# One value product of 256 columns for both parts of the attention weights, and attention outputs stored as two parts in block order

## The chip, the cores and the metric

The kernel runs as one launch on one core of a Trainium2 chip. The metric is the device time of that launch in microseconds; of several runs the median is taken. A profile is one further execution, recorded by the hardware profiler. Engines are called as in the profile: PE (TensorE, products), PEld (its weight loads), DVE (VectorE), ACT (ScalarE), POOL (GpSimd), SP (SyncE, which here only issues DMAs).

## What is computed

One layer of a hybrid encoder on 1024 tokens (a grid of 16 rows of 64) with 1024 channels: a half feed-forward step, a token mixer of two branches (neighbourhood attention and a state-space model, SSM), a second half feed-forward step, an embedding step and a final norm. All of it is float32. The change lies in the attention branch and, with a few lines, in the final norm. Cut to these:

```python
def neighbourhood_attention(q, k, v, rpb):        # 8 heads of 64 channels
    def row_block(r):
        rs = jnp.clip(r - wh // 2, 0, rows - wh)                   # window of 8 rows
        kr = lax.dynamic_slice_in_dim(kg, rs, wh, axis=1)
        vr = lax.dynamic_slice_in_dim(vg, rs, wh, axis=1)
        kn = kr[:, :, col_idx]                                     # 16 columns for each query
        vn = vr[:, :, col_idx]
        ...
        sc = jnp.einsum('bchd,brcwhd->bhcrw', qr, kn) * scale + bias[None]
        pr = jax.nn.softmax(sc, axis=-1)...
        return jnp.einsum('bhcrw,brcwhd->bchd', pr, vn)
...
        y_attn = neighbourhood_attention(q, k, v, na_rpb[i]) @ w_attn_out[i]
        y_ssm = s5_branch(s_in, ...) @ w_ssm_out[i]
        h = h + (g_attn * y_attn + g_ssm * y_ssm) @ w_out[i]
...
    return rms_norm(h, final_norm)
```

## The kernel before

**Products in two parts.** Operands of the large products are split into a high part, rounded to the type float32r, and a low part, the rest. A product is then the sum of high x high, high x low and low x high, three products in one accumulator (`mm3`, L183 to L186; `split`, L152 to L154, writes the high part on ACT and the low part on DVE).

**The mixer.** Two streams of work are woven together on PE. The outer one is a plain sequence of projections: the SSM input, the values (stored to v_d), then for each pair of heads the queries and keys (`qk_proj`) and the gates (`gate_tile`, L1360). After each `mm3` it calls `tick()`. The inner one is the generator `mixer_side` (L1287), which hands out a piece of attention or of the SSM each time its count of ticks has run out. PE executes in the order in which the program is written; the other engines' instructions are put in order by a scheduler.

**Attention.** A unit is one head, one half of the grid's rows (rb) and one of four column blocks (cb) of 16 columns: 128 queries against 12 rows of 24 or 32 keys. There are 8 x 2 x 4 = 64 units. Round j of the loop at L1319 does four things in this order: the scores of unit j (`attn_scores`: two products into the tile s, the table added and the minimum taken on DVE, the exponential and its scaling on ACT), the transposes of unit j - 3 (`attn_turn`: three on PE into the tile pt, then the high part pth by ACT and the low part ptl by DVE), the value products of unit j - 5 (`attn_values`), and two steps of the SSM scan on POOL. From round 48 on (SO) it adds the SSM outputs: `ssm_out` copies states out of the scan's array (xs, L1111) and three rounds later runs products into yo. A round ends with 4 ticks (from 48 on 3), that is 12 (9) products of 512 columns of the outer stream.

The value products need high x high, high x low and low x high. PE's loaded operand holds 64 high and 64 low columns of the values (vhl), so one product with pth over these 128 columns gives high x high in partitions 0 to 63 and low x high in 64 to 127; a second one with ptl, over the 64 high columns alone, adds high x low to the former:

```python
            T.matmul(O[:, ksl(cb)], lhsT=hl[0:kp, rb + g].rearrange("p h d -> p (h d)"), rhs=ph[0:kp, ksl(g)], start=(g == 0), stop=False,
            T.matmul(O[0:64, ksl(cb)], lhsT=hl[0:kp, rb + g, 0], rhs=pl[0:kp, ksl(g)], start=False, stop=(g == 2),
```

With three groups g of four rows that is six products a unit. O is one PSUM bank (of 8, all under one tag) for four units; after the fourth, ACT copies its lower half out (ol), DVE adds the halves in row order (ot), and ACT's queue stores 64 x 512 numbers to o_d, of shape 512 x 1024.

**Reading the outputs back.** When the inner stream has ended, `load_br` (L1400) reads o_d (b = 0) and the SSM branch's y2_d (b = 1) for the two halves t of the tokens, through buffers "st" (three, 1024 columns each) and "tmp" (four, 512 columns), and splits them into bh and bl for the products br (`branches`). Between these reads SP issues those of the residual (hbuf from h_d), of the weights (wst from in_was) and stores of gates (g_d).

**Buffers.** While the mixer runs, "w" (12 of 1024 columns) holds weights, queries and keys, "x" (56 of 512 columns) everything else of that width.

**The end.** `end` (L1675) writes the last quarter of the embedding and the final norm by hand: the order on DVE and ACT there is that of the program. `stat` gathers the squares on PE (ms), `rstd` (L205) makes the reciprocal root from ms, `scaled` (L1654) multiplies by the last gain on ACT, `finish` multiplies and stores.

## Time and profile before

| | |
|---|---|
| time, median of 3 runs | 2098.58 us (2096.72 to 2100.43) |
| time of the profiled execution | 2096.29 us |
| span of the profiled execution | 2094.5 us, 28063 instructions |
| mean granted TensorE clock | 0.998 |
| attention units (value products) | 851.7 to 1104.5 us of the span |
| HBM read, written | 201.01 MB, 82.31 MB |

The span is the time from the first to the last instruction; the execution's own time also holds what lies around it, 1.8 us. The page cuts the span into 40 equal slices of 52 us; a digit is the busy share of a slice in tenths, so that the mixer is to be seen in the middle, from where POOL works a second time (the SSM scan):

```profile
PE   8999999999999999999999999999999999999998
DVE  7897776667967334677753668995665665786855
ACT  6434333334445333667774635643333334445543
POOL 0037556441000006888200001000000000000000
```

A row of a tile or of a line gives the number of instructions, the shortest, median and longest duration in ns and the first and last start in us. A row of the timeline gives start, duration, engine, line, operation, out<-in, and in brackets the idle time before it and what ended it. Starts of products lie closer together than their durations, since products are pipelined.

### The profile page before, as it was taken

What the parts mean: (1) busy time and instruction counts of PE and PEld (TensorE: products, weight loads), DVE (VectorE), ACT (ScalarE), POOL (GpSimd) and SP (SyncE); (2) the same over time, 40 slices, a digit from 0 to 9 for tenths busy, and PEclk for the clock granted to TensorE, in tenths of its full rate; (3) what the DMA queues carried; (4) which work ended last, traced back from release to release, by engine and by line L of the source; (5) the groups of instructions that cost most, each with busy time, mean ns of one, the idle gap of its engine ahead of it and who ended that gap; (6) DMA issues with size and microseconds to landing.
All of it is one profiled execution on the core that took longest, in us unless ns stands there. A gap on an engine that the chain in (4) does not pass through costs nothing.

```text
span 2094.5 us, 28063 instructions
## 1 busy us (share of the span) xinstructions
PE 2074.5 (99%) x9662; PEld 1705.4 (81%) x9662; DVE 1416.1 (68%) x2420; ACT 999.6 (48%) x1832; POOL 399.4 (19%) x636
## 2 busy tenths in 40 slices
PE   8999999999999999999999999999999999999998
PEld 3788888888888888888898888788888888888886
DVE  7897776667967334677753668995665665786855
ACT  6434333334445333667774635643333334445543
POOL 0037556441000006888200001000000000000000
PEclk9999999999999999999999999999999999999999
DMA  3435444475533551233477745243324238433302
GB/s 134 143 118 154 125 135 120 144 270 169 188 114 111 159 189 64 70 97 98 123 208 260 247 145 117 77 150 121 100 86 135 82 121 297 155 106 94 118 21 81
DMA packets 197744, 285.19 MB, mean 136 GB/s; under 512 B 41569, under 2 KB 81121, under 8 KB 197601
## 3 DMA queue, kind: packets, MB, share of 16 engines
q1 hardware_dynamic: 180304, 258.20, 38.8%
q10 hardware_dynamic: 14992, 21.00, 3.0%
q0 software_dynamic: 2304, 4.20, 1.2%
q8 instruction: 76, 1.25, 0.2%
q14 instruction: 68, 0.55, 0.1%
HBM read 201.01 MB, written 82.31 MB: 135 GB/s over the span
## 4 chain that ended last, share of the span: by engine, by line
PE 94%; DVE 2%; ACT 1%; DMA 1%; SPq 0%; issue 0%; DVEq 0%; ACTq 0%
PE dx L184 4%; PE dx L185 4%; PE dx L186 4%; PE gx L184 3%; PE ux L184 3%; PE ux L186 3%; PE gx L186 3%; PE gx L185 3%; PE ux L185 3%; PE gt L184 3%; PE gt L185 3%; PE gt L186 3%; PE dy L186 2%; PE dy L184 2%; PE dy L185 2%; PE gy L184 2%
## 5 line engine op out<-in xcount | busy, mean ns | idle before, releaser
L153 ACT CAST wh<-hbuf 128x512 fp32r<-128x512 f32 x280 | 173.0, 622 | 392.3 <-PE gx L185 80.9
L154 DVE TENSOR_TENSOR wl<-hbuf,wh 128x512 fp32r<-128x512 f32 x280 | 209.2, 750 | 122.7 <-ACT wh L153 120.5
L153 ACT CAST wh<-wblk 128x512 fp32r<-128x512 f32 x190 | 118.0, 622 | 192.6 <-PE dx L185 83.2
L154 DVE TENSOR_TENSOR wl<-wblk,wh 128x512 fp32r<-128x512 f32 x190 | 130.6, 690 | 49.3 <-ACT wh L153 41.8
L184 PE MATMUL dx<-ah,wh 128*128 128x512 f32 x416 | 163.3, 393 | 0.3 <-DVE hbuf L688 0.3
L186 PE MATMUL dx<-ah,wl 128*128 128x512 f32 x416 | 161.9, 389 | 0.0
L185 PE MATMUL dx<-al,wh 128*128 128x512 f32 x416 | 161.8, 389 | 0.0
L1092 POOL TENSOR_TENSOR sc<-X,rho 128x128 f32<-128x128 f32 x128 | 77.9, 609 | 327.2 <-ACT X L1075 317.3
L154 DVE TENSOR_TENSOR al<-araw,ah 128x512 fp32r<-128x512 f32 x154 | 106.3, 694 | 50.1 <-PE dx L185 21.1
L184 PE MATMUL gx<-xh,wh 128*128 128x512 f32 x320 | 124.9, 390 | 1.2 <-DVE c L575 1.2
L184 PE MATMUL ux<-xh,wh 128*128 128x512 f32 x320 | 125.0, 390 | 0.0
L186 PE MATMUL ux<-xh,wl 128*128 128x512 f32 x320 | 124.5, 389 | 0.0
L185 PE MATMUL gx<-xl,wh 128*128 128x512 f32 x320 | 124.5, 389 | 0.0
L186 PE MATMUL gx<-xh,wl 128*128 128x512 f32 x320 | 124.5, 389 | 0.0
L185 PE MATMUL ux<-xl,wh 128*128 128x512 f32 x320 | 124.5, 389 | 0.0
L153 ACT CAST ah<-araw 128x512 fp32r<-128x512 f32 x154 | 94.9, 619 | 43.2 <-PE dx L185 12.6
L184 PE MATMUL gt<-xh,wh 128*128 128x512 f32 x256 | 102.7, 401 | 0.0
L186 PE MATMUL gt<-xh,wl 128*128 128x512 f32 x256 | 99.8, 390 | 0.0
L185 PE MATMUL gt<-xl,wh 128*128 128x512 f32 x256 | 99.8, 390 | 0.0
L422 DVE TENSOR_TENSOR hbuf<-hbuf 128x512 f32<-128x512 f32 x120 | 91.4, 762 | 2.1
L184 PEld LDWEIGHTS dx<-ah,wh 128*128 128x128 f32 x416 | 78.1, 188 | 17.8 <-issue 0.7
L185 PEld LDWEIGHTS dx<-al,wh 128*128 128x128 f32 x416 | 78.1, 188 | 16.9 <-issue 0.7
(381 smaller groups left out, 5590.2 us busy)
## 6 DMA issues: line engine op xcount, KB each, us to landing
araw<-a_d SPq DMA_DIRECT2D x154, 256.0 KB
a_d<-c SPq DMA_DIRECT2D x148, 256.0 KB
wblk<-in_wd SPq DMA_DIRECT2D x88, 256.0 KB
hbuf<-in_wg SPq DMA_DIRECT2D x40, 512.0 KB
hbuf<-in_wu SPq DMA_DIRECT2D x40, 512.0 KB
wst<-in_win SPq DMA_DIRECT2D x26, 512.0 KB
hbuf<-in_xT SPq DMA_DIRECT2D x32, 256.0 KB
h_d<-hbuf ACTq DMA_DIRECT2D x32, 256.0 KB
```

Source lines behind the costliest of these rows:

```text
L153: A.copy(hi, src)
L154: return eng.tensor_tensor(lo, src, hi.bitcast(F32), ALU.subtract)
L184: T.matmul(o, lhsT=wh, rhs=xh, start=first, stop=False, skip_group_check=more)
L185: T.matmul(o, lhsT=wh, rhs=xl, start=False, stop=False, skip_group_check=more)
L186: T.matmul(o, lhsT=wl, rhs=xh, start=False, stop=last, skip_group_check=more)
L422: V.tensor_tensor(b11, (b12, b22, None, None, b21)[i - 2], b11, ALU.subtract)
L1092: G.tensor_tensor(sc, both, rho4, ALU.mult)
```

## The change

**One product for both parts.** `attn_turn` writes the high and the low part of the transposed weights side by side into one tile ptb (three groups of 2 x 128 columns, two buffers). `attn_values` loads all 128 columns of vhl and streams 256 columns in one product a group: three a unit. It also gives low x low, which is not used.

**Two column blocks in a bank.** O is a bank for two units now, each with 256 columns; 32 banks are taken instead of 16. After the second unit ACT copies the columns that belong to the high part (all 128 partitions) into ot, DVE adds the high x low part to partitions 0 to 63, and ot is stored as it is: 2 x 64 x 256 numbers to o_d, which is 2 x 512 x 1024 now, in the order of the column blocks. The sum of the two halves and the order by rows are made when it is read back: `load_br` reads both halves into two "st" buffers, adds them on DVE, and the split reads the sum in the changed order.

**Order in a round.** The value products stand ahead of the transposes.

**Buffers.** The queries are kept in 512-wide buffers, one for each half of the tokens, and "w" has 10 buffers instead of 12.

**The end.** In the last `stat`, the two scalings come after the reciprocal root on ACT (`mid`).

```diff
     v_d = dtile("v_d", [SEQ, 512])
-    o_d = dtile("o_d", [512, SEQ])
+    o_d = dtile("o_d", [2, 512, SEQ])
     g_d = dtile("g_d", [16, P, SEQ])
...
-    def rstd(m, r, q):
+    def rstd(m, r, q, mid=None):
         A.activation(r, m, AF.Abs_reciprocal_sqrt, bias=eps)
+        if mid is not None:
+            mid()
         V.tensor_tensor(q, r, r, ALU.mult)
...
-        def stat(self, r=None, summed=False):
+        def stat(self, r=None, summed=False, mid=None):
             if summed:
...
             r = thid("rs", [P, self.n], F32) if r is None else r
-            rstd(m, r, q)
+            rstd(m, r, q, mid)
             self.r = r
...
     ap_ = ap_cm.__enter__()
-    cur.update(st=(ap_, "st", 3), w=(ap_, "w", 12), tmp=(ap_, "tmp", 4))
+    cur.update(st=(ap_, "st", 3), w=(ap_, "w", 10), tmp=(ap_, "tmp", 4))
...
             for i in range(2):
-                if t == 0:
-                    qs.append(tw("qs"))
+                q = thid("qs")
+                qs.append(q)
                 src = o[i * 64:(i + 1) * 64].rearrange("p (r b c) -> p r b c", r=8, b=4)
...
                 def view(sl):
-                    return qs[i][sl, hsl(t)].rearrange("p (b r c) -> p r b c", b=4, r=8)
+                    return q[sl].rearrange("p (b r c) -> p r b c", b=4, r=8)
                 A.copy(view(hs), src)
...
         for i in range(2):
-            qkv[2 * hp + i] = (qs[i], kh[i], kl[i])
+            qkv[2 * hp + i] = (qs[i::2], kh[i], kl[i])
...
         nk = 12 * n
-        qv = q[:, rb * HT + cb * P:rb * HT + (cb + 1) * P]
+        qv = q[rb][:, ksl(cb)]
...
             T.transpose(tp[0:kp, ksl(g)], sm[:, g * kp:(g + 1) * kp], ident)
-        ph = thid("pth", [P, 384])
-        pl = thid("ptl", [P, 384])
-        A.copy(ph[0:kp], tp[0:kp, 0:384])
-        V.tensor_tensor(pl[0:kp], tp[0:kp, 0:384], ph[0:kp].bitcast(F32), ALU.subtract)
-        return ph, pl
-    def attn_values(hd, rb, cb, O, ph, pl):
+        pb = ap_.tile([P, 3, 2, P], F32R, tag="ptb", bufs=2, name="ptb")
+        src = tp[0:kp, 0:384].rearrange("p (g q) -> p g q", g=3)
+        A.copy(pb[0:kp, :, 0], src)
+        V.tensor_tensor(pb[0:kp, :, 1], src, pb[0:kp, :, 0].bitcast(F32), ALU.subtract)
+        return pb
+    def attn_values(hd, rb, cb, O, pb):
         kp = 4 * KNC[cb]
         hl = vld[hd, cb]
+        o = O["o"][:, (cb % 2) * 256:(cb % 2) * 256 + 256]
         for g in range(3):
-            T.matmul(O[:, ksl(cb)], lhsT=hl[0:kp, rb + g].rearrange("p h d -> p (h d)"), rhs=ph[0:kp, ksl(g)], start=(g == 0), stop=False,
+            T.matmul(o, lhsT=hl[0:kp, rb + g].rearrange("p h d -> p (h d)"), rhs=pb[0:kp, g].rearrange("p h q -> p (h q)"), start=(g == 0), stop=(g == 2),
                      skip_group_check=True)
-            T.matmul(O[0:64, ksl(cb)], lhsT=hl[0:kp, rb + g, 0], rhs=pl[0:kp, ksl(g)], start=False, stop=(g == 2),
-                     skip_group_check=True)
-        if cb == 3:
-            ot, ol = tmp("ot"), tmp("ol")
-            A.copy(ol[0:64], O[64:128])
-            V.tensor_tensor(ot[0:64].rearrange("p (r b c) -> p b r c", r=8, b=4),
-                            O[0:64].rearrange("p (b r c) -> p b r c", b=4, r=8),
-                            ol[0:64].rearrange("p (b r c) -> p b r c", b=4, r=8), ALU.add)
-            nc.scalar.dma_start(o_d[hd * 64:(hd + 1) * 64, hsl(rb)], ot[0:64])
+        if cb % 2 == 0:
+            return
+        ot = ap_.tile([P, 256], F32, tag="ot", bufs=2, name="ot")
+        ov = ot.rearrange("p (b q) -> p b q", b=2)
+        src = O["o"].rearrange("p (b h q) -> p h b q", b=2, h=2)
+        A.copy(ov, src[:, 0])
+        V.tensor_tensor(ov[0:64], src[0:64, 1], ov[0:64], ALU.add)
+        nc.scalar.dma_start(o_d[:, hd * 64:(hd + 1) * 64, rb * HT + (cb - 1) * P:rb * HT + (cb + 1) * P], ot)
...
                 sms[j] = attn_scores(hd, rb, cb)
+            if 0 <= j - 5 < n:
+                hd, rb, cb = units[j - 5]
+                if cb % 2 == 0:
+                    O.setdefault((hd, rb), {})["o"] = bank("O")
+                attn_values(hd, rb, cb, O[hd, rb], pts.pop(j - 5))
+                if rb == 1 and hd + 1 < NH:
+                    load_v(hd + 1, cb)
             if 0 <= j - 3 < n:
                 pts[j - 3] = attn_turn(units[j - 3][2], sms.pop(j - 3))
-            if 0 <= j - 5 < n:
-                hd, rb, cb = units[j - 5]
-                if cb == 0:
-                    O[hd, rb] = bank("O")
-                attn_values(hd, rb, cb, O[hd, rb], *pts.pop(j - 5))
-                if rb == 1 and hd + 1 < NH:
-                    load_v(hd + 1, cb)
             scan_steps(2)
...
             for k in range(0, 4, 2):
-                st = tst("br")
-                nc.sync.dma_start(st.rearrange("p (k c) -> p k c", k=2),
-                                  o_d[k * P:(k + 2) * P, hsl(t)].rearrange("(k p) c -> p k c", p=P))
+                st = [tst("br") for _ in range(2)]
+                for w in range(2):
+                    nc.sync.dma_start(st[w].rearrange("p (k c) -> p k c", k=2),
+                                      o_d[w, k * P:(k + 2) * P, hsl(t)].rearrange("(k p) c -> p k c", p=P))
+                V.tensor_tensor(st[0], st[0], st[1], ALU.add)
                 for i in range(2):
                     hi, lo = tx("bh"), tx("bl")
-                    split(hi, lo, st[:, hsl(i)])
+                    sv = st[0][:, hsl(i)].rearrange("p (b r c) -> p r b c", b=4, r=8)
+                    hv, lv = (x.rearrange("p (r b c) -> p r b c", b=4, r=8) for x in (hi, lo))
+                    split(hv, lv, sv)
                     res.append((hi, lo))
...
         A.activation(dummy, eps, AF.Abs_reciprocal_sqrt)
-        scaled(6, six[3])
         added(a, b, s, hm)
         fin[2].square(7, V)
-        scaled(7, hm)
         finish(1, (4, 6))
-        fin[2].stat()
+        fin[2].stat(mid=lambda: (scaled(6, six[3]), scaled(7, hm)))
         finish(2)
```

What the change moves on PE shows in any round of the middle: s are the scores of unit j, pt the transposes of unit j - 3, O the value products of unit j - 5, gt a gate product of the outer stream. Before, around one round:

```order
L1207 MATMUL s<-kh,qs 128x288
L1208 MATMUL s<-kl,qs 128x288
L1223 MATMUL pt<-ident,sm 96x128 x3
L1235 MATMUL O<-pth,vhl 128x128
L1237 MATMUL O<-ptl,vhl 64x128
L1235 MATMUL O<-pth,vhl 128x128
L1237 MATMUL O<-ptl,vhl 64x128
L1235 MATMUL O<-pth,vhl 128x128
L1237 MATMUL O<-ptl,vhl 64x128
L184 MATMUL gt<-xh,wh 128x512
L185 MATMUL gt<-xl,wh 128x512
```

And now, at the same place:

```order
L1209 MATMUL s<-kh,qs 128x288
L1210 MATMUL s<-kl,qs 128x288
L1239 MATMUL O<-ptb,vhl 128x256 x3
L1225 MATMUL pt<-ident,sm 96x128 x3
L184 MATMUL gt<-xh,wh 128x512
L185 MATMUL gt<-xl,wh 128x512
```

Six products of 128 columns have become three of 256, and they have moved from behind the transposes to behind the scores; what follows the transposes is the outer stream's product of 512 columns.

On SP's queue, where the outputs are read back (g_d are stores of gates, wst the second block of the weights in_was, br the reads of o_d and then of y2_d). Before, up to the first read of y2_d:

```order
L1364 DMA g_d_82<-gs_11180 128x512
L1364 DMA g_d_82<-gs_11254 128x512
L1427 DMA wst_11416<-in_was 128x1024
L1406 DMA br_11506<-o_d_81 128x2x512
L1406 DMA br_11516<-o_d_81 128x2x512
L1364 DMA g_d_82<-gs_11315 128x512
L1416 DMA br_11426<-y2_d_84 128x8x64
```

And now, from the last read of o_d for the first half of the tokens:

```order
L1412 DMA br_11216<-o_d_81 128x2x512
L1369 DMA g_d_82<-gs_11070 128x512
L1436 DMA wst_11228<-in_was 128x1024
L1436 DMA wst_11238<-in_was 128x1024
L1412 DMA br_11328<-o_d_81 128x2x512
L1412 DMA br_11329<-o_d_81 128x2x512
L1369 DMA g_d_82<-gs_11131 128x512
L1412 DMA br_11341<-o_d_81 128x2x512
L1412 DMA br_11342<-o_d_81 128x2x512
L1425 DMA br_11248<-y2_d_84 128x8x64
```

Both weight blocks and four reads of o_d for the second half now stand in one row ahead of the first y2_d read; each takes an "st" buffer that an earlier one has to leave.

On DVE at the same stage (wl is the low part of those weights, sg the last step of the SSM branch's gate ahead of its store to y2_d, bl the low part of what is read back). Before:

```order
L154 TENSOR_TENSOR wl_11423<-wst_11416,wh_11422 128x512
L1281 TENSOR_TENSOR sg_11331<-sg_11331,yg_11047 128x512
L1281 TENSOR_TENSOR sg_11348<-sg_11348,yg_11058 128x512
L1281 TENSOR_TENSOR sg_11365<-sg_11365,yg_11069 128x512
L1281 TENSOR_TENSOR sg_11382<-sg_11382,yg_11080 128x512
L154 TENSOR_TENSOR bl_11428<-br_11426,bh_11427 128x512
```

And now:

```order
L154 TENSOR_TENSOR wl_11245<-wst_11238,wh_11244 128x512
L1414 TENSOR_TENSOR br_11328<-br_11328,br_11329 128x1024
L1286 TENSOR_TENSOR sg_11147<-sg_11147,yg_10863 128x512
L1286 TENSOR_TENSOR sg_11164<-sg_11164,yg_10874 128x512
L1414 TENSOR_TENSOR br_11341<-br_11341,br_11342 128x1024
L1286 TENSOR_TENSOR sg_11181<-sg_11181,yg_10885 128x512
L1286 TENSOR_TENSOR sg_11198<-sg_11198,yg_10896 128x512
L154 TENSOR_TENSOR bl_11250<-br_11248,bh_11249 128x512
```

The two adds of the second half stand ahead of the first and of the third of these four sg steps.

## The prediction, made before the changed kernel ran

> **What bounds the kernel now.** I read the page's busy times and its chain of work first, then the windows of the stage that the change touches, then PE's waits there.
>
> ```profile
> PE 2074.5 (99%) x9662; PEld 1705.4 (81%) x9662; DVE 1416.1 (68%) x2420; ACT 999.6 (48%) x1832; POOL 399.4 (19%) x636
> PE 94%; DVE 2%; ACT 1%; DMA 1%; SPq 0%; issue 0%; DVEq 0%; ACTq 0%
> ```
>
> TensorE (PE) is busy 99% of the span and carries 94% of the chain that ended last: time leaves the kernel only where PE's stream gets shorter. The next view gives, by stage: length, then busy us (instructions) of PE, PEld, DVE, ACT, POOL, then clock, DMA share, GB/s.
>
> ```profile
> 870.00:920.00 50.00, 50.00 (x299) 43.50 (x297) 37.91 (x90) 35.45 (x79) 43.11 (x89) 1.00 0.29 81
> 1020.00:1070.00 50.00, 49.33 (x335) 44.39 (x335) 30.43 (x91) 37.48 (x93) 0.00 (x0) 1.00 0.66 193
> 1110.00:1150.00 40.00, 40.00 (x178) 33.14 (x177) 14.24 (x21) 19.63 (x30) 0.00 (x0) 1.00 0.80 287
> ```
>
> The attention runs here (870), then attention beside the SSM outputs (1020), then the stage that reads the attention outputs back (1110). PE has no idle time in the first and last and 0.67 us in the second; DVE is at 76% and ACT at 71% in the first. PE's waits between 1015 and 1110 us are two, 1.1 us in all:
>
> ```profile
> PE yo L1117 <- DVE ot L1242: 0.7, 1, 0.7
> PE yo L1117 <- DMA emi<-u_d: 0.4, 1, 0.4
> ```
>
> So a shorter PE stream should shorten the span by as much, unless an operand becomes late.
>
> **The value products.** A unit's six value products follow its three transposes; after them comes a product of 512 columns. First the tile O's row, then the timeline of one unit (start us, duration; durations are pipelined, so I count from start to start).
>
> ```profile
> L1235 PE MATMUL O<-pth,vhl x192: 220/276/306, 851.7 to 1104.5; 96*128 96x128 f32 x96, 128*128 128x128 f32 x96
> ```
>
> ```profile
> 859.21 0.49 PE L1223 MATMUL pt<-ident,sm 128*96 128x128 f32 x3
> 859.46 0.31 PE L1235 MATMUL O<-pth,vhl 128*128 128x128 f32 x1
> 859.60 0.22 PE L1237 MATMUL O<-ptl,vhl 128*64 128x128 f32 x1
> 859.66 0.28 PE L1235 MATMUL O<-pth,vhl 128*128 128x128 f32 x1
> 859.77 0.22 PE L1237 MATMUL O<-ptl,vhl 128*64 128x128 f32 x1
> ...
> 860.01 0.45 PE L184 MATMUL q<-xh,wh 128*128 128x512 f32 x1
> 860.29 0.39 PE L185 MATMUL q<-xl,wh 128*128 128x512 f32 x1
> ```
>
> There are 192 / 3 = 64 units. From the first value product to the second 512-column product are 860.29 - 859.46 = 0.83 us. Inside, a start follows 0.11 us after a product with 128 weight columns and 0.06 us after one with 64, although both stream the same 128 columns: the weight loads set this pace, not the streaming. The early units have transposes but no value products yet, and show what a 512-column product costs directly behind transposes:
>
> ```profile
> 844.65 0.49 PE L1223 MATMUL pt<-ident,sm 128*96 128x128 f32 x3
> 844.89 0.48 PE L184 MATMUL gt<-xh,wh 128*128 128x512 f32 x1
> 845.21 0.39 PE L185 MATMUL gt<-xl,wh 128*128 128x512 f32 x1
> 845.44 0.40 PE L186 MATMUL gt<-xh,wl 128*128 128x512 f32 x1
> ```
>
> That is 0.32 us instead of the usual 0.23. The kernel's end has products of 256 columns with a full weight load before each, the shape that the change makes:
>
> ```profile
> 2067.61 0.28 PE L185 MATMUL pg<-xl,whh 128*128 128x256 f32 x1
> 2067.73 0.28 PE L186 MATMUL pg<-xh,whl 128*128 128x256 f32 x1
> ```
>
> They start 0.12 us apart. After the change the products stand behind the scores and ahead of the transposes, so a unit pays 3 x 0.12 = 0.36 us for them, and 0.32 us for the 512-column product behind the transposes: 0.68 us for 0.83, **0.15 us less, and 9.6 us over 64 units**. Bounds: with 0.28 us (860.01 to 860.29) in place of 0.32 it is 0.19 us a unit, 12.2 us; with the longest spacing of today's value products (0.14 us, 859.46 to 859.60) for each of the three, 0.83 - 0.42 - 0.32 = 0.09 us, 5.8 us. I take 0.12 us, from the rows of the same shape.
>
> [...] The rows above say 120 ns.
>
> **What stands beside PE.** Outputs are now taken out of PSUM 32 times instead of 16, in 256 columns:
>
> ```profile
> L1241 ACT COPY ol<-O x16: 582/583/587, 864.6 to 1107.0; 64x512 f32<-64x512 f32 x16
> L1242 DVE TENSOR_TENSOR ot<-O,ol x16: 671/683/683, 865.2 to 1107.6; 64x512 f32<-64x512 f32 x16
> L1245 ACTq DMA_DIRECT2D o_d<-ot x16: 452/453/507, 865.9 to 1108.3; - x16
> ```
>
> ```profile
> 2081.06 0.38 ACT L1684 ACTIVATE ps<-pg 128x256 f32<-128x256 f32 x1
> 2081.82 0.41 DVE L1651 TENSOR_TENSOR ps<-ps,pp 128x256 f32<-128x256 f32 x1
> ```
>
> ACT: 32 x 0.38 - 16 x 0.583 = +2.8 us, and 16 more store issues of 0.45 us, +7.2 us in its queue. DVE: 32 x 0.41 - 16 x 0.683 = +2.2 us. Over the 253 us of the O row that is 4% of ACT and 1% of DVE; with each unit about 4% shorter too, ACT goes from 71% to some 78% and DVE from 76% to some 80%. PE hides it, so I cost it at nothing; were ACT to set the pace, the price would be up to the 10.0 us. The two halves of a weight tile are written by an ACT cast and a DVE subtract of the same 384 columns as now: no change. A value product now waits for both halves, where the first needed only ACT's; but they are made two units (some 8 us) before, so the wait is covered. The queries move from the 1024-wide weight buffers to 512-wide ones, and that pool shrinks from 12 to 10: two leave and two go, nothing.
>
> PE reaches the SSM outputs earlier, by 43 units x 0.15 = 6.5 us at the first; the POOL scan doesn't run faster:
>
> ```profile
> L1092 POOL TENSOR_TENSOR sc<-X,rho x128: 495/528/1774, 798.3 to 1008.9; 128x128 f32<-128x128 f32 x128
> ```
>
> ```profile
> L1111 ACT COPY xs<-X x32: 388/403/409, 1015.3 to 1080.3; 64x256 f32<-64x256 f32 x32
> ```
>
> The scan ends at about 1010.4 and its first reader starts at 1015.3; 6.5 us earlier it would wait 1.6 us. Behind it on ACT stand exponentials whose transposes come three units (11 us) later: no cost.
>
> At the very end, rsqrt is moved ahead of two scalings on ACT:
>
> ```profile
> 2084.57 0.89 ACT L1655 ACTIVATE hbuf<-hbuf,gains 128x256 f32<-128x256 f32 x2
> 2084.60 0.70 PE L251 MATMUL ms<-sq,ones 128*128 128x256 f32 x2 [0.70 <-DVE sq L232]
> 2085.37 0.45 ACT L205 ACTIVATE rs<-ms,eps 128x256 f32<-128x256 f32 x1
> ```
>
> Its operand ms is ready at 2085.30 and it started at 2085.37: at most 0.07 us, and the scalings hide behind DVE's steps. Nothing.
>
> **Reading the outputs back.** o_d doubles: 2 MB more are written over the attention and 2 MB more read. The reads pass through "st", three buffers: ten loads use it now instead of six, and the order shows the last two attention reads between the freeing of buffers and the y2 reads on SP, with four adds of 1024 columns on DVE. On the time axis of before:
>
> ```profile
> 1140.83 0.33 SPq L1427 DMA_DIRECT2D wst<-in_was  x1
> ```
>
> ```profile
> 1144.36 0.62 ACT L153 CAST wh<-wst 128x512 fp32r<-128x512 f32 x1 [0.75 <-DMA wst<-in_was]
> 1155.33 0.69 DVE L1281 TENSOR_TENSOR sg<-sg,yg 128x512 f32<-128x512 f32 x1 [1.98 <-ACT sg L1280]
> 1169.35 1.29 DVE L154 TENSOR_TENSOR bl<-br,bh 128x512 fp32r<-128x512 f32 x2 [0.28 <-ACT bh L153]
> ```
>
> ```profile
> L184 PE MATMUL br<-bh,wh x32: 389/389/389, 1168.0 to 1189.1; 128*128 128x512 f32 x32
> ```
>
> Such a load takes 1144.36 - 1140.83 = 3.5 us. Three of them now follow one another, each waiting for a buffer of the last: was at about 1141.5, ready 1145 and split by 1147; an attention read, 1150.5, added by 1151.7 (two 0.6 us halves, an estimate from the 1169.35 row); another, 1155.2, added by 1156.4. The sg step behind that add (the last but one of four, 2.8 us apart) started at 1155.33, so about 1 us late. The y2 reads and the splits of the second half queue behind these steps. The second half's attention tiles were split by 1169.35 + 1.29 = 1170.6, and their last product starts at 1168.0 + 33 x 0.23 = 1175.6 (two groups of 12 ahead of it, then 9): 4.9 us of cover. Cost nothing; with loads twice as slow (7 us, my other end) the last add ends at 1141.5 + 7 + 2 + 7 + 1.2 + 7 + 1.2 = 1166.9, the last sg step behind it at 1168.3 instead of 1158.8, 9.5 us late, and PE waits 9.5 - 4.9 = 4.6 us.
>
> **Sum.** -9.6 us. The profiled execution took 2096.29 us (span 2094.5), which makes 2086.7; the median of the runs, 2098.58, lies 2.3 us above it, so the forecast for the median is **2089.0 us**.
>
> **Rivals.**
>
> *The readback chain turns into PE's wait.* Place: the first br products of the second half. Each us by which a load is slower costs 3 us. From 7 us (4.6 us lost) the whole saving is gone at 8.7 us, and the kernel is measurably slower from 10.1 us on; at 11 us it would be 2098.6 - 9.6 + 16.6 = 2105.6. For it speaks a DMA share of 0.80 in that stage; against it that the readback starts when the heavy loads are mostly over. 0.05 for beyond 10.1 us.
>
> *The weight load is not hidden.* If a 128-column load (0.11 us) had to end before its product could stream, a value product would cost 0.23 us: 0.69 + 0.32 - 0.83 = +0.18 us a unit, 11.5 us, 2110 us. The 0.12 us between 256-column products with such a load each speaks against it. 0.02. [...]
>
> *The saving is partly lost.* Units 48 to 63 run beside DMA at 0.66 and already show waits for emi; if DMA sets their pace, 16 x 0.15 = 2.4 us go, 2091.4. With the low bound of the product, or 7 us loads, on top, 2094 to 2097. 0.15.
>
> *It does not do what it says.* The order shows three products a unit, ahead of the transposes; left is only that an operand is late in every unit, for instance DVE's half of the weights. DVE idles 24% of the time, so hardly; 2098.6. 0.03.
>
> **How the numbers follow.** The forecast between its product bounds (2086.4 to 2092.8) gets 0.67, still more saved (PE's two waits gone too, 2083.5 to 2086) 0.08. The range from 2083.5 to 2097.0 takes in both ends and the partial loss. A measurement of this kernel tells some 0.2% (4.2 us) from no change: faster by more 0.80 (the forecast, more saved, and a third of the partial loss), within it 0.13, slower 0.07.
>
> **What would show it.** Right: O<-ptb products 0.12 us apart, the 512-column product behind transposes 0.32 us, each unit 0.15 us shorter, the last O about 9.5 us earlier, PE's waits there still near 1 us. Wrong: O products at 0.14 or 0.23 us; PE waiting for DVE ptb or ot, for emi, or for bl at the br products; the stage from the last O to the first br longer than now.

## The result, and the profile after

| | before | after |
|---|---|---|
| time, median of the runs | 2099.31 us (4 runs, 2096.72 to 2100.43) | 2118.9 us (4 runs, 2118.16 to 2123.82) |
| the profiled execution: its time, its span | 2096.29 us, 2094.5 us | 2118.6 us, 2116.8 us |
| unit 0: first score product s | 835.2 us | 837.0 us |
| unit 48: the same | 1018.3 us | 1014.4 us |
| first glu product | 1123.1 us | 1138.2 us |
| first br product | 1168.0 us | 1184.1 us |
| last br product | 1254.8 us | 1277.4 us |
| last ms product | 2084.9 us | 2107.6 us |

The changed kernel is slower: ratio 1.0101, 95% interval 1.0089 to 1.0114, some 20 us. The forecast was 2089.0 us and 2097.0 us the end of its range. The table's lower rows (starts in the two traces) say where. Up to unit 48 the change gains (177.4 us from unit 0 for 183.1 before). From unit 48 to glu it loses 19.0 us (123.8 for 104.8), at the br products another 6.5 us (93.3 for 86.8). Behind them nothing changes (830.2 and 830.1 us); 1.8 us come ahead of unit 0 and 1.0 between glu and br.

First the page of after: busy time, and the shares of the chain of work that ended last.

```profile
PE 2077.4 (98%) x9470; PEld 1703.1 (80%) x9470; DVE 1421.4 (67%) x2440; ACT 996.3 (47%) x1848; POOL 402.2 (19%) x636
PE 75%; POOL 9%; DMA 6%; DVE 5%; issue 2%; ACT 2%; SPq 1%; DVEq 0%; ACTq 0%; POOLq 0%
```

PE still has the span nearly filled, but the chain says something new: PE had 94% of it, now 75%, and POOL 9% and DMA 6%, which had none and 1%. Busy time alone would have hidden this, since a product that runs at a lower clock is counted busy for longer (a 512-column product 0.63 us at a granted clock of 0.50, 0.39 at 1.00, in after at 1019.52 and 1020.51 us). The windows of the same stages (length; busy us and instructions of PE, PEld, DVE, ACT, POOL; granted clock, DMA share, GB/s):

```profile
870.00:920.00 50.00, 50.00 (x267) 43.25 (x266) 36.93 (x89) 34.84 (x83) 42.90 (x91) 1.00 0.32 99
1020.00:1070.00 50.00, 43.31 (x241) 38.22 (x240) 24.97 (x74) 29.75 (x76) 0.00 (x0) 0.90 0.57 161
1110.00:1150.00 40.00, 38.99 (x182) 31.82 (x181) 12.02 (x18) 20.20 (x31) 0.00 (x0) 1.00 0.70 220
```

The early units run as predicted, PE full at full clock. In the window from 1020 PE issued 241 instructions where it had issued 335, with 6.7 us of idle time in place of 0.67 and a clock of 0.90 in place of 1.00. DMA is busier there by neither measure: a share of 0.57 for 0.66, 161 GB/s for 193. So the bandwidth of all 16 engines together isn't what runs out. PE's longest waits between 1005 and 1290 us (in all, times, longest):

```profile
PE yo L1119 <- DMA emi<-u_d: 8.7, 7, 2.8
PE br L184 <- ACT bh L153: 3.9, 1, 3.9
PE s L1209 <- DVE stat L1213: 2.9, 1, 2.9
PE s L1210 <- DVE kl L1160: 2.0, 1, 2.0
PE br L185 <- DVE bl L154: 0.7, 1, 0.7
```

All nine kinds of wait in that stretch make 19.8 us; before, the waits were 1.1 us. And SP's waits for landings of o_d stores between 1014 and 1125 us, before (the first two rows) and after:

```profile
SPq L1167 <- DMA o_d<-ot: 0.8, 1, 0.8
SPq L1364 <- DMA o_d<-ot: 0.3, 1, 0.3
```

```profile
SPq L1104 <- DMA o_d<-ot: 7.7, 2, 4.3
SPq L1169 <- DMA o_d<-ot: 7.2, 3, 3.9
SPq L1105 <- DMA o_d<-ot: 5.1, 2, 3.6
```

SP issues loads that have nothing to do with o_d: emi (L1104, L1105) and the values vf (L1169). Before the issue it waited 20 us in all for stores to land, where it had waited 1.1.

The term of the sum itself came true, as the timeline of one unit shows (start, duration):

```profile
860.68 0.29 PE L1210 MATMUL s<-kl,qs 128*128 128x288 f32 x1
860.81 0.52 PE L1239 MATMUL O<-ptb,vhl 128*128 128x256 f32 x3
861.17 0.49 PE L1225 MATMUL pt<-ident,sm 128*96 128x128 f32 x3
861.41 0.48 PE L184 MATMUL q<-xh,wh 128*128 128x512 f32 x1
861.73 0.39 PE L185 MATMUL q<-xl,wh 128*128 128x512 f32 x1
```

Three value products take 861.17 - 860.81 = 0.36 us, the 512-column product behind the transposes 0.32 us, both as predicted. Over the 40 undisturbed units between 850 and 1010 us, the time from a unit's first score product to the first 512-column product behind it fell from 1.105 to 0.915 us, and the twelve 512-column products between two units grew from 2.78 to 2.84 us (the 0.32 now lies among them): 0.13 us less a unit, 8.3 us over 64. The question is what took 28 us.

### The profile page after: what moved, and what is told of

Read it like the earlier page. It is cut to its first block, busy times and chain, and to the rows that moved or that the text cites. A ratio compares the mean times of both kernels' runs of the same rounds, so it can differ in the third digit from the quotient of the medians.

```text
span 2116.8 us, 27743 instructions
## 1 busy us (share of the span) xinstructions
PE 2077.4 (98%) x9470; PEld 1703.1 (80%) x9470; DVE 1421.4 (67%) x2440; ACT 996.3 (47%) x1848; POOL 402.2 (19%) x636
## 4 chain that ended last, share of the span: by engine, by line
PE 75%; POOL 9%; DMA 6%; DVE 5%; issue 2%; ACT 2%; SPq 1%; DVEq 0%; ACTq 0%; POOLq 0%
PE dx L184 4%; PE dx L186 4%; PE dx L185 4%; POOL sc L1094 4%; PE ux L184 3%; PE ux L185 3%; PE ux L186 3%; PE gx L184 3%; PE gx L186 3%; PE gx L185 3%; POOL X L1096 3%; POOL sc L1095 2%; PE dy L185 2%; PE dy L184 2%; PE dy L186 2%
## 5 line engine op out<-in xcount | busy, mean ns | idle before, releaser
L153 ACT CAST ah<-araw 128x512 fp32r<-128x512 f32 x154 | 94.8, 619 | 48.6 <-PE dx L185 12.5
```

The source lines that it names most:

```text
L153: A.copy(hi, src)
```

## The experiments

Three suspects: **STORE**, something in the new stores; **SCAN**, POOL's scan, which PE now reaches before it ends; **READBACK**, the doubled loads of o_d. Behind the first stands a further question, what it is in the stores (count, bytes, queue, shape). Each ratio is to the kernel before, in runs on the same chip. The scheduler orders the other engines anew with each edit, so a run's order can differ in more than the edit; what rests on one such difference alone is said to.

### Parts of the change alone (e1, e2)

e1 keeps the products and takes back the stores and the readback (the readback's lines are left out here):

```diff
-    o_d = dtile("o_d", [2, 512, SEQ])
+    o_d = dtile("o_d", [512, SEQ])
...
+        A.copy(lv[0:64], hi[64:128])
+        V.tensor_tensor(lv[0:64], lo[0:64], lv[0:64], ALU.add)
+        V.tensor_tensor(ov, hi[0:64], lv[0:64], ALU.add)
+        if cb == 3:
+            nc.scalar.dma_start(o_d[hd * 64:(hd + 1) * 64, hsl(rb)], ot[0:64])
```

> The 256-column value products alone; the two halves are added on the chip (two VectorE additions of 64x256 and a 64x256 copy per two units) and stored and read back as in the kernel before (16 stores of 64 rows x 512, one readback of each block). Theory STORE (the 32 stores of 128 rows in the SSM units delay the loads queued on SyncE behind them, and the doubled readback delays br): the whole loss of 20 us and the 9.6 us saving appear, 2088 to 2093 us, TensorE waits for emi and for bh/bl near those of before. Theory SCAN (GpSimd's scan ends at about 1013 us and the faster units reach the first xs copies before it; kl and sm wait behind xs on VectorE): the wait of TensorE for kl at unit 48 stays at about 2 us and most of the loss between unit 48 and glu stays, only the br part (7.5 us) goes: 2106 to 2112 us. Theory READBACK (the doubled readback alone costs more than it saved): also 2111 us, but with unit 48 to glu as long as in the changed kernel.

Measured: 2098.64 us, ratio 1.0001 (0.9992 to 1.0010). It lies between what STORE and SCAN expected: the 20 us are gone, but so is the saving. PE's waits for emi are 0.6 us and br waits for nothing, as STORE said; one wait of another kind is left, larger than in the changed kernel (PE's waits of e1, and the row of the scan's first operation: ns min/median/max, first and last start):

```profile
PE s L1210 <- DVE kl L1160: 7.8, 1, 7.8
```

```profile
L1094 POOL TENSOR_TENSOR sc<-X,rho x128: 491/530/2580, 799.4 to 1018.7; 128x128 f32<-128x128 f32 x128
```

And DVE's timeline there:

```profile
1011.04 1.21 DVE L154 TENSOR_TENSOR wl<-wst,wh 128x1024 fp32r<-128x1024 f32 x1
1018.62 0.81 DVE L1113 COPY xs<-X 64x256 f32<-64x256 f32 x2 [6.36 <-POOL X L1096]
...
1020.55 1.38 DVE L1160 SCALAR_TENSOR_TENSOR kl<-k,kh 64x512 fp32r<-64x512 f32 x2
```

DVE is done at 1012.3, stands before the first xs copy until POOL's scan gives it its columns at 1018.6, and only behind the copies writes kl, the low part of the next heads' keys, for which PE has waited since 1014.2. The scan ended later than before (last row start 1018.7 for 1008.9) and PE came earlier. So e1 would have the product's saving, and SCAN takes it back; e5 tests that. (The profiled execution of e1 took 2101.08 us, 2.4 more than the median, so its wait may be longer than usual.)

e2 is the reverse: the kernel before, with the changed kernel's stores and readback.

```diff
-        if cb == 3:
-            ot, ol = tmp("ot"), tmp("ol")
...
+        if cb % 2 == 1:
+            ot = tmp("ot", [P, 256])
+            A.copy(ot, O[:, (cb - 1) * P:(cb + 1) * P])
+            nc.scalar.dma_start(o_d[:, hd * 64:(hd + 1) * 64, rb * HT + (cb - 1) * P:rb * HT + (cb + 1) * P], ot)
```

> The stores and the readback alone: value products, transposes and their split as in the kernel before, but both halves of a bank are copied out for two column blocks at a time, stored as 32 stores of 128 rows x 256 in block order and read back twice and added, as in the changed kernel. Theory STORE: slower than the kernel before by what the stores and the readback cost, 15 to 26 us: 2114 to 2125 us, with SyncE waiting for landings of o_d stores in units 48 to 63. Theory SCAN: unit 48 comes later than the scan's end as in the kernel before, so only the readback part appears: 2100 to 2107 us. Theory READBACK: 2106 us, with the br part 7.5 us longer and the stage before it as in the kernel before.

Measured: 2135.85 us, ratio 1.0180 (1.0163 to 1.0197), 37 us slower, beyond what STORE expected. SP waits 27.8 us for o_d between 1010 and 1125 us. Here ot also takes buffers of "tmp", which vf needs, so a slow store is paid for twice, and the size isn't that of the changed kernel. The sign is plain: stores and readback together cost the time, without the new products. e7 and e9 tell them apart.

### Later xs copies, another queue (e3, e4)

```diff
-        SO = 48
+        SO = 50
```

> The changed kernel with the first SSM output at unit 50 in place of 48, so that its first xs copies come about 7 us after the scan's end. Theory SCAN: the wait for kl at the first xs unit goes and with it the late chain behind it: 8 to 18 us faster than the changed kernel, 2101 to 2111 us. Theory STORE or READBACK: within 3 us of the changed kernel (2116 to 2122 us), since stores and readback are the same.

Measured: 2112.07 us, ratio 1.0062 (1.0047 to 1.0077): 7 us better than the changed kernel, between the two ranges, and not by the way expected. The scheduler put the xs copies ahead of kl as before, and PE still waited 3.5 us for kl, and 7.8 us for emi. A miss as a test of SCAN: moving a step in the program did not move it on the engine that mattered.

```diff
-        nc.scalar.dma_start(o_d[:, hd * 64
+        (nc.gpsimd if hd >= 6 else nc.scalar).dma_start(o_d[:, hd * 64
```

> The changed kernel with the o_d stores of the last two heads (8 of 32, units 48 to 63) issued by GpSimd, which is idle after its scan, in place of ScalarE. Theory STORE: SyncE no longer waits for landings of these stores, TensorE's waits for emi (8.7 us) and for sm behind vhl (2.9 us) mostly go: 2103 to 2112 us. Theory SCAN or READBACK: within 3 us of the changed kernel, 2116 to 2122 us.

Measured: 2119.38 us, ratio 1.0096 (1.0080 to 1.0112), no change; waits for emi 9.8 us. SP's waits for o_d fell from 20 to 4.7 us, so neither ACT's queue nor the eight stores' hold on SP explains it. But for DMAs that POOL issues the profile gives the time from issue to landing (row: KB each, median us):

```profile
o_d<-ot POOLq DMA_DIRECT2D x6, 128.0 KB, 6.9
```

6.9 us for 128 KB, on a queue of POOL's that carried nothing else then (the row has the six of these stores issued in that stretch). That is what led on.

### xs behind the exponentials; count, readback (e5 to e8)

e5 and e8 put the xs copies behind the same unit's work on their engine, in e1 and in the changed kernel:

```diff
-                (A.copy if g == r else V.tensor_copy)(xs[r * 64:(r + 1) * 64, g], both)
+                with tc.issue_after(last["a" if g == r else "d"].ins):
+                    (A.copy if g == r else V.tensor_copy)(xs[r * 64:(r + 1) * 64, g], both)
```

> As e1_sum_on_chip (256-column products, halves added on the chip, stores and readback of before), but the copies xs of each SSM unit are put behind the same unit's exponentials (ScalarE) and score reductions (VectorE) in the engines' order, so that kl of the next heads no longer stands behind a copy that waits for the scan. Theory SCAN: the 7.8 us wait for kl at unit 48 and the low clock after it go, and the product's saving appears: 2088 to 2092 us, faster than before by 0.3 to 0.5%. Rival (the product brings nothing over the whole stage, the wait only collected slack): 2096 to 2099 us.

Measured: 2094.42 us, ratio 0.9984 (0.9975 to 0.9993). The wait for kl is gone, though the scan ends as late as in e1 (1018.9 and 1020.1 us), and the kernel is faster than before, by less than expected. SCAN holds for e1.

e6 is e5 with two stores of 64 x 256 in place of one of 64 x 512:

```diff
-        if cb == 3:
-            nc.scalar.dma_start(o_d[hd * 64:(hd + 1) * 64, hsl(rb)], ot[0:64])
+        nc.scalar.dma_start(o_d[hd * 64:(hd + 1) * 64, rb * HT + (cb - 1) * P:rb * HT + (cb + 1) * P], ot[0:64])
```

> As e5_sum_behind, but each sum is stored in two stores of 64 rows x 256 in block order in place of one of 64 x 512: the same bytes in twice as many DMAs (32 in place of 16), read back once. Theory STORE by count (a DMA more on the semaphores that the loads of SyncE wait on in turn): 8 to 14 us slower than e5, waits of TensorE for emi of 5 us or more. Theory STORE by bytes or by what else hangs on them: within 3 us of e5.

Measured: 2093.82 us, ratio 0.9979 (0.9970 to 0.9988), as e5; waits for emi 0.7 us. The count of the stores costs nothing that shows.

e7 is e5 with each block of o_d read twice:

```diff
+                V.tensor_tensor(st, st, st2, ALU.max)
```

> As e5_sum_behind, but every block of o_d is read back twice into two buffers and the two are joined by a maximum on VectorE (which leaves the value), as the changed kernel reads two parts and adds them. Theory READBACK: the first br products wait for bh and bl, the stage from glu to the end of br grows by 6 to 8 us: 6 to 8 us slower than e5, nothing before glu. Theory STORE (the br wait of the changed kernel came from the late end of the stage before it): within 2 us of e5.

Measured: 2096.38 us, ratio 0.9991 (0.9982 to 1.0000): 2.0 us more than e5, less than expected, and not clear of noise, since the two intervals overlap. The traces show where it would be: PE waits 2.1 us for bh and 0.7 for bl, where e5 has neither wait, and the br stage takes 91.7 us for 86.8.

> The changed kernel with the copies xs behind the same unit's exponentials and reductions, as in e5. Theory SCAN alone: the whole loss from unit 48 to glu goes, 2097 to 2104 us. Theory SCAN and STORE and READBACK together: only the 2.0 us wait for kl and the low clock behind it go, 2112 to 2117 us, and the waits for emi stay at 6 to 10 us.

Measured: 2118.98 us, ratio 1.0104 (1.0088 to 1.0119), no change, a miss for both expectations. The wait for kl is gone and others have its place: for emi 12.5 us in place of 8.7. A cause can be removed and gain nothing as long as a larger one behind it sets the end; here that one is STORE, as e10 shows below.

### The shape of the store's target (e9, e11, e12, e14)

What is odd about a store of 128 KB that takes 6.9 us? The trace records when each DMA's semaphore is raised. Between two issues on one semaphore the traces of before and after have 16 raises for every DMA but two kinds, 5 for each of the 128 vf loads and, in after, 3 for each of the 32 stores of o_d, so the raises between two issues are taken to belong to the first of them. Counted and timed like this, between 1014 and 1125 us (issue to last raise):

```
                target of one store        raises   o_d median (n)   vf max   emi<-u_d max
before          64 x 512                     16       2.9 us (6)      3.5 us     4.4 us
after           2 x 64 x 256                  3       6.4 us (10)     6.6 us     5.8 us
e6              64 x 256                     16       2.8 us (11)     4.0 us     4.6 us
e9              128 x 256                    16       2.8 us (11)     3.7 us     4.5 us
e12             2 x 32 x 512                  3       6.6 us (6)      6.7 us     6.4 us
e14             64 x 256, twice              16       3.0 us (22)     3.3 us     5.0 us
```

Stores of before and after carry the same 128 KB. But the changed kernel's target, `o_d[:, hd * 64:(hd + 1) * 64, ...]`, begins with a dimension of 2, and its semaphore is raised 3 times instead of 16. The vf loads, whose source begins with a dimension of 4, raise theirs 5 times in every kernel of the table. In the table the time goes with the count: 6.4 and 6.6 us for stores with 3 raises, 2.8 to 3.0 for those with 16. The trace's records of single packets point the same way. On ACT's queue, the store that the changed kernel issues at 1019.88 us is 128 packets of 1024 bytes and 2 of 4 bytes; never more than 4 are under way at once, and they take 5.0 us. That of the kernel before at 1022.70 us is 64 packets of 2048 bytes and 16 of 4 bytes, up to 16 at once, and takes 2.2 us. That such a store is carried by few of the 16 engines, as SHAPE has it below, is an estimate from these counts (3 raises where the other has 16, at most 4 packets under way where the other has 16). No trace names the engine of a packet.

e9 alters the layout of o_d, and the readback so far as it must follow (8 loads of 64 rows a half where there were 4 of 128; not shown):

```diff
-    o_d = dtile("o_d", [2, 512, SEQ])
+    o_d = dtile("o_d", [8, P, SEQ])
...
-        nc.scalar.dma_start(o_d[:, hd * 64:(hd + 1) * 64, rb * HT + (cb - 1) * P:rb * HT + (cb + 1) * P], ot)
+        nc.scalar.dma_start(o_d[hd, :, rb * HT + (cb - 1) * P:rb * HT + (cb + 1) * P], ot)
```

> The changed kernel with one thing altered: the scratch tensor o_d is laid out as [8 heads, 128, 1024] in place of [2 parts, 512, 1024], so that a store's 128 rows of 256 columns go to 128 rows of one block in place of 2 blocks of 64 rows (same bytes, same count; the readback takes 8 loads of 64 rows where it took 4 of 128 for each half of the sequence). Theory SHAPE (a store whose target begins with a dimension of 2 is carried by few of the 16 DMA engines: in the changed kernel it took a median of 6.4 us to land between 1014 and 1125 us, with 3 counts on its semaphore, where the 64-row stores of the kernel before took 2.9 us with 16 counts; the loads behind it on those engines and on its semaphore are late): the stores land in 2 to 4 us, TensorE's waits for emi fall from 8.7 to 3 us or less, and the time falls by 8 to 14 us to 2105 to 2111 us. Theory BYTES (twice the bytes stored cost the time): within 3 us of the changed kernel, 2116 to 2122 us.

Measured: 2102.21 us, ratio 1.0017 (1.0008 to 1.0026): 16.7 us better than the changed kernel, more than expected, with the same bytes in the same count of stores. SP's waits for o_d, and PE's between 1005 and 1290 us:

```profile
SPq L1369 <- DMA o_d<-ot: 2.6, 1, 2.6
SPq L1169 <- DMA o_d<-ot: 1.4, 2, 1.2
SPq L1105 <- DMA o_d<-ot: 1.3, 1, 1.3
```

```profile
PE br L184 <- ACT bh L153: 5.4, 1, 5.4
PE s L1210 <- DVE kl L1160: 3.2, 1, 3.2
PE yo L1119 <- DMA emi<-u_d: 0.9, 1, 0.9
```

The waits for emi fall from 8.7 to 0.9 us. What is left are the other two suspects, kl and bh. e11 is e9 with e4's queue, to have the landing from the profile itself:

```diff
+        (nc.gpsimd if hd >= 6 else nc.scalar).dma_start(o_d[hd, :, rb * HT + (cb - 1) * P:rb * HT + (cb + 1) * P], ot)
```

> As e9, with the stores of the last two heads issued by GpSimd as in e4, so that the profile gives their time from issue to landing by itself. Theory SHAPE: a median of 2 to 4 us in place of the 6.9 us of e4. Theory BYTES: 6 us or more.

```profile
o_d<-ot POOLq DMA_DIRECT2D x8, 128.0 KB, 3.2
```

3.2 us for 6.9, same bytes, same queue (2102.58 us, one run). e12 goes the other way: the kernel before, with its stores' targets split in two, and with 16 loads of 32 rows in the readback in place of 4 of 128 (not shown).

```diff
-    o_d = dtile("o_d", [512, SEQ])
+    o_d = dtile("o_d", [2, 256, SEQ])
...
-            nc.scalar.dma_start(o_d[hd * 64:(hd + 1) * 64, hsl(rb)], ot[0:64])
+            nc.scalar.dma_start(o_d[:, hd * 32:(hd + 1) * 32, hsl(rb)], ot[0:64])
```

> The kernel before with the target of its 16 stores (64 rows x 512, same bytes, same places in the program) split into two blocks of 32 rows, o_d being [2, 256, 1024]; the readback takes 16 loads of 32 rows in place of 4 of 128 rows. Products, sums and buffers are those of before. Theory SHAPE: the stores land in 5 to 7 us, SyncE waits for them and TensorE for emi, and the kernel becomes slower than before by 4 to 12 us, 2103 to 2111 us. Theory BYTES: within 2 us of before.

Measured: 2108.99 us, ratio 1.0048 (1.0034 to 1.0062). 16 stores with a bad target cost the old kernel 11 us:

```profile
SPq L1167 <- DMA o_d<-ot: 7.1, 2, 4.5
SPq L1364 <- DMA o_d<-ot: 4.4, 1, 4.4
```

Half of the expectation failed: PE waits only 0.5 us for emi. Its longest waits are 3.4 us for ot and 2.6 us for stat, on DVE. There ot takes buffers of "tmp", as in e2, and between 1014 and 1110 us ACT waits 9.4 us for vf and 5.3 us for landings of o_d (2.4 and 2.4 in the kernel before). So the slow stores reach PE by other waits than in the changed kernel. The loss lies in the same stage: from unit 48 to glu 116.1 us, 104.9 in the kernel before.

Last, the changed kernel with its layout kept and each store written as two:

```diff
-        nc.scalar.dma_start(o_d[:, hd * 64:(hd + 1) * 64, rb * HT + (cb - 1) * P:rb * HT + (cb + 1) * P], ot)
+        for w in range(2):
+            nc.scalar.dma_start(o_d[w, hd * 64:(hd + 1) * 64, rb * HT + (cb - 1) * P:rb * HT + (cb + 1) * P], ot[w * 64:(w + 1) * 64])
```

> The changed kernel, o_d unchanged as [2, 512, 1024], with each store of 128 rows written as two stores of 64 rows, one to each part: 64 stores in place of 32, same bytes, same places. Theory SHAPE (one DMA whose target begins with a dimension of 2 is carried by few engines): each lands in 2 to 4 us and the time is near that of e9, 2099 to 2106 us. Theory PLACE (the two distant blocks make the store slow) or COUNT: no faster than the changed kernel, 2115 to 2125 us.

Measured: 2092.72 us, ratio 0.9976 (0.9965 to 0.9987). The same two blocks, reached by 64 DMAs in place of 32, and 26 us faster: neither the two places nor the count made the store slow, but the one DMA over both. Of PE's waits between 1005 and 1290 us one is left, the wait for kl and those at br are gone:

```profile
PE yo L1119 <- DVE stat L1217: 2.9, 1, 2.9
```

It is faster than SHAPE expected. With this run alone it can't be said how much of that is due to the stores and how much to the order that came with the edit; e14's loads of o_d are 4 a half where e9's are 8, too. For the wait for kl the trace has a reason: the scan ends at 1011.7 us, ahead of unit 48 (1014.2), where the changed kernel's ended at 1014.7.

### The order of the readback (e10, e13, e15)

e10 is e9 with e5's order of the xs copies.

> As e9, and the copies xs behind the same unit's exponentials and reductions, as in e5. Theories SHAPE and SCAN and READBACK together: 2096 to 2102 us, what is left against e5 (2094.4 us) being the doubled readback, 2 to 6 us. Theory BYTES: 2113 to 2119 us.

Measured: 2094.64 us, ratio 0.9984 (0.9975 to 0.9993), 7.6 us better than e9 and better than expected. Now that the stores are out of the way, the same edit that gained nothing in e8 brings its share. What is left is at br; PE's wait there and ACT's timeline before it ends (the profiled execution took 2097.8 us, 3.2 more than the median):

```profile
PE br L184 <- ACT bh L153: 6.1, 1, 6.1
```

```profile
1164.08 2.31 ACT L153 CAST bh<-br 128x512 fp32r<-128x512 f32 x2 [1.12 <-DVE sg L1288]
1167.36 1.05 ACT L153 CAST bh<-br 128x512 fp32r<-128x512 f32 x1 [0.96 <-DMA br<-y_d]
1169.48 2.09 ACT L153 CAST bh<-br 128x512 fp32r<-128x512 f32 x3 [0.59 <-DMA br<-y_d]
```

PE waits from 1165.05 to 1171.1 for splits of o_d's second half. The x2 and x1 rows and the first of the x3 row are splits of y2, 1.1 us each, which wait for y2's loads; the wanted ones (0.6 us) stand behind them on ACT, the first two as the rest of the x3 row. Their data had been added on DVE by 1159.4. e13 writes that readback ahead of y2's:

```diff
+    oy[1].append(load_br(1, 0))
     oy[0].append(load_br(0, 1))
...
-    for b in range(2):
-        oy[1].append(load_br(1, b))
+    oy[1].append(load_br(1, 1))
```

> As e10, with the readback of o_d for the second half of the sequence written ahead of the readback of y2 for the first half, so that its splits (bh, bl) stand ahead of those that wait for y2's loads on ScalarE and VectorE. In e10 the third group of br products (second half, o_d) waits 6.1 us for a split that stands behind the y2 splits. Theory ORDER: that wait goes and the clock behind it recovers, 5 to 9 us faster than e10: 2086 to 2090 us. Theory LOADS (twice the loads cost the time, whatever the order): the wait moves to the first products of y2, 2092 to 2096 us.

Measured: 2089.93 us, ratio 0.9963 (0.9951 to 0.9976), the best version found, with all of its readback still doubled. PE's waits between 1130 and 1260 us:

```profile
PE br L184 <- DVE gt L1519: 1.1, 1, 1.1
PE br L185 <- DVE bl L154: 0.3, 1, 0.3
```

ORDER holds: the br stage takes 88.9 us for e10's 96.7, though a part of that difference belongs to the long execution in which e10 was profiled. e13 also still has the smaller pool "w" and the queries in their new buffers, so these cost nothing that shows.

e15 joins e14's stores with both edits of order.

> e14's two stores of 64 rows, with e10's order of the xs copies and e13's order of the readback. If the three causes are independent: e14 less its one wait of 2.9 us for emi at best and with no wait at br, 2086 to 2090 us. If the other two were consequences of the slow stores: as e14, 2091 to 2094 us.

Measured: 2092.99 us, ratio 0.9979 (0.9970 to 0.9988), as e14: with e14's stores the other two waits weren't there to be removed. One wait of 3.0 us for yo at 1041.8 us keeps it behind e13; its cause wasn't followed.

## Why the prediction was wrong, point by point

- **"0.15 us less, and 9.6 us over 64 units": right in kind, a little large.** Spacings as predicted, 0.13 us a unit, 8.3 us in place of 9.6. e13, with the same products and PE's waits nearly gone, is 7.6 us faster than the kernel before on its chip.
- **The step that failed: "16 more store issues of 0.45 us, +7.2 us in its queue", "cost it at nothing".** A store was priced by its issue, never by its landing. The target was in the diff: `[2, 512, SEQ]`, stored to with one DMA over the leading 2. It lands in 6.4 us instead of 2.9, and behind it come late the loads of emi (longest 5.8 us for 4.4) and vf (6.6 for 3.5) and with them PE. Size: 16.7 us by e9 against the changed kernel, 11 us for half as many stores in e12.
- **"Behind it on ACT stand exponentials whose transposes come three units (11 us) later: no cost": wrong engine.** The coming wait for the scan was seen, and its cover was looked up on ACT alone. Half of the xs copies run on DVE, and there kl stood behind them, which PE needs at once. Size: 2.0 us of wait in the changed kernel, 7.8 in e1; 7.6 us by e10 against e9.
- **The readback: the right place and the right wait, and a price that came out equal by luck.** The rival saw that late loads would hold up the y2 reads and the splits of the second half. It said "with loads twice as slow (7 us, my other end)" that PE waits 4.6 us, and PE waited 3.9 + 0.7 = 4.6 us. But the three loads from which it is worked out did not take 7 us. They are the first three rows here; the reads of the first half, which the sum left out, took 5.8 to 7.4 us each, and the last of them was issued only when the one before it had landed (the last two rows; all from the chain of after; start, duration):

```profile
1164.30 3.50 DMA wst<-in_was
1169.80 3.95 DMA br<-o_d
1175.12 5.08 DMA br<-o_d
```

```profile
1148.52 7.00 DMA br<-o_d
1155.58 7.44 DMA br<-o_d
```

The value chosen, 3.5 us, was that of one weight load at 1140; the four o_d loads of the kernel before had taken 6.7, 8.9, 4.7 and 5.2 us in its trace, and were not looked up. The second half's last sum was there at 1181.5 us, but its first split started at 1192.9, behind four splits of y2 on ACT. That order is what turned the late loads into PE's wait (e13).
- **The third rival ("The saving is partly lost", 2.4 us) saw the place and not the size.** Waits for emi grew from 0.4 to 8.7 us, and not because DMA as a whole "sets their pace": its share fell from 0.66 to 0.57 in the window from 1020 us.
- The remaining steps held: the weight load is hidden (0.12 us between value products), ACT and DVE did not become the bound in the early units, and the moves in the final norm changed nothing that shows (last br to last ms 830.2 us after, 830.1 before).

Taken away one after the other, the three causes lead from 2118.9 to 2102.2 (e9) to 2094.6 (e10) to 2089.9 us (e13). By the ratios, which leave out what the chips differ (the kernel before took 2098.03 us on that of e9 and e10, 2097.54 on that of e13), the steps are 17.6, 6.9 and 4.4 us. The shares depend on the order in which they are taken, as e8 shows. Not settled: whether the loads of emi were late mostly because SP waited for a semaphore that a slow store held, or because they themselves took longer beside it. e4, where six of the ten late stores were not on ACT's queue and SP waited only 4.7 us for o_d, speaks for the latter. So does the longest of the changed kernel's waits, 2.8 us until 1057.33: the emi load it waited for was issued at 1051.37, 1.6 us behind a store, and took 5.8 us to land, where the median is 3.5.

## What to carry to other kernels

Price a new store by its landing time and by who is queued behind it, and look at the first dimension of its DRAM side: one of 2 cost this kernel 17 us, and a layout with 128 rows took it back, as did two DMAs of 64 rows. When a step is going to wait, look at what stands behind it on every engine that executes a part of it. If a removed wait gains nothing, look for a larger one behind it before the theory is dropped: the same edit was worth 0 in e8 and 7.6 us in e10.

## What the runs showed of the hardware

**A slow store delays others, not only itself.** For its own data the store had time: o_d is read only after the stage. Its cost (16.7 us by e9) came through loads that had nothing to do with it, emi (longest 5.8 us for 4.4) and vf (6.6 for 3.5), while the DMA share fell from 0.66 to 0.57.

**PE's clock after a short wait.** After 2.8 us without work PE does not resume at full pace (timeline of after, 512-column products; the 4 us from 1057 have a granted clock of 0.59), nor behind the 2.0 us wait for kl:

```profile
1016.63 0.53 PE L1210 MATMUL s<-kl,qs 128*128 128x288 f32 x1 [1.95 <-DVE kl L1160]
...
1018.67 0.63 PE L185 MATMUL gt<-xl,wh 128*128 128x512 f32 x1
1019.09 0.63 PE L186 MATMUL gt<-xh,wl 128*128 128x512 f32 x1
...
1057.33 0.46 PE L1119 MATMUL yo<-emi 128*128 128x128 f32 x2 [2.80 <-DMA emi<-u_d]
...
1058.83 0.63 PE L185 MATMUL gt<-xl,wh 128*128 128x512 f32 x1
1059.26 0.63 PE L186 MATMUL gt<-xh,wl 128*128 128x512 f32 x1
...
1061.27 0.40 PE L185 MATMUL gt<-xl,wh 128*128 128x512 f32 x1
1061.51 0.40 PE L186 MATMUL gt<-xh,wl 128*128 128x512 f32 x1
```

```profile
1057.00:1061.00 4.00, 3.67 (x13) 3.12 (x14) 2.28 (x7) 1.70 (x5) 0.00 (x0) 0.59 0.79 231
```

Starts are 0.43 us apart, and 0.23 again some 4 us after the wait. The seven steps from the start at 1058.26 to that at 1061.27 us take 3.01 us instead of 7 x 0.23 = 1.61, so the wait of 2.8 us costs at least 4.2. In the changed kernel the granted clock is 0.50 in four stretches between 1016 and 1198 us, 17 us in all, in which PE is busy for 16; the kernel before and e13 have no such stretch there (mean granted clock 0.998 each, 0.994 in the changed kernel). At half the clock these 16 us do the work of 8 (an estimate from these figures). With the 18.7 us by which the waits grew that is 26.7, nearly all of the 28 us. Behind the wait of 2.8 us the clock was 0.50 from 1057.71 us on, behind the 2.0 us wait for kl from 1016.75 us on, for 3.4 us each time.

**The scan's pace.** By and large the scan took longer the more additions DVE had for the attention outputs. From its first step to its end it took 207.6 us in e2 (none), 211.9 and 212.6 us in the kernel before and in e12 (one for two pairs of units), 211.7 to 216.8 us in the changed kernel and its relatives (one a pair), and 218.1 to 220.7 us in e1, e5, e6 and e7 (two a pair). That DVE's work slows POOL's is a guess from this; no run tested it alone.
